# Shared decay-row buffers, 16-bit level masks and a reordered start in a DeltaNet and differential-attention block

## The chip, the cores and the metric

The kernel runs on one core of a Trainium2 chip. The metric is the device time of one execution in microseconds (us). The program is built by a scheduler: the Python code issues instructions, and the scheduler sets the order in which each engine's queue holds them, from its own estimate of when each could start. On the chip every engine takes its queue strictly in that order, so an instruction whose input is late holds up all that stands behind it on the same engine.

Engines are named as in the profile: PE (TensorE, matmuls), PEld (its weight loads), DVE (VectorE), ACT (ScalarE), POOL (GpSimd), SP (which here only issues DMAs). Names such as SPq or ACTq stand for the DMA-issuing instructions of an engine's queue.

## The reference, cut to what matters

Two layers over 256 context tokens and 256 latent tokens of width 2048. Layer 0 mixes tokens with a gated DeltaNet in both directions, layer 1 with differential attention. Each layer starts with a norm whose result is shifted and scaled by vectors that come from two large matrix products (the modulation).

```
for i in range(DEPTH):                                  # 2 layers
    mod_l = silu_c @ ada_w[i] + ada_b[i]                # shift, scale, gate: 3 x 2048
    mod_c = silu_cc @ ada_w[i] + ada_b[i]
    h_lat = rmsnorm(x, norm_w[i]) * (1.0 + sc_l) + sh_l
    h_ctx = rmsnorm(ctx, norm_w[i]) * (1.0 + sc_c) + sh_c
    ...                                                 # mixer, then x = x + gt_l * out_lat
...
lower = jnp.where(strict, jnp.einsum('nbhid,nbhjd->nbhij', kb, kc) * decay, 0.0)
tinv = lax.linalg.triangular_solve(eye + lower, ...)    # per chunk, head and direction
a_intra = jnp.einsum('nbhid,nbhjd->nbhij', qc, kc) * decay
def step(s, inp):                                       # one chunk
    v_new = u_i - w_i @ s
    o_i = q_i @ s + a_i @ v_new
    s = s * gl_i[..., None, None] + jnp.einsum('bhck,bhcv->bhkv', k_i, v_new)
```

`decay` is exp of the difference of two cumulated log gates, one per pair of tokens of a chunk. The kernel multiplies it into two kinds of matrices: k times k (to be inverted) and k times q (the attention inside a chunk).

## The kernel before, in words

**The start (lines 283 to 328).** 16 tiles of x, `xt`, 256 KB each, are loaded. ACT squares them (lines 299, 302), DVE sums them into `acc0` (line 303), `rstd_rows` (lines 203 to 214) turns the sum into a row `rrow0` by two matmuls into the psum tag `iv`, with a small power on POOL between them. The shift and scale vectors come from `ada_pair` (lines 173 to 182): 32 matmuls per pair of column blocks, over four 512 KB tiles `ar` of the modulation weight that SP loads (`ada_load`, line 169) into a ring of eight buffers; 16 pairs, 64 loads, 33.5 MB. A loop over eight steps takes two pairs, scales two tiles of x (`make_h`, lines 216 to 224: POOL, ACT, ACT, DVE), and feeds three early projections `ba`, `k0`, `q0` (lines 312 to 326). Before this stage's end SP also issues small constants and four stores that fill the DRAM scratch `tu_d` with zeros from a tile `zt` (line 466).

**The gates (`gates`, lines 361 to 457)** turn the projection `ba` into cumulated log gates, and store them as rows in DRAM, `gc_d` (line 435).

**The DeltaNet stage** works through 16 groups `g` of four states (two heads, two directions), four chunks of 128 tokens in two halves. Python generators yield in an order that a small planner (`Drive`) sets by priorities; the scheduler then orders the engines.

- `decay` (lines 682 to 695) makes a decay tile: two DMAs on SP copy rows of `gc_d` to all 128 partitions of a tile of 128 x 512 (line 686), four DVE instructions subtract and cap (line 692), one ACT instruction takes exp (line 694). It is called with the tag `grm` for the matrices to be inverted and with `gra` for the attention matrices. Each tag has one buffer, so the next load under a tag waits for line 700 of the last one.
- `scaled` (line 699: product of the matmul in psum `gq` and a mask, `gm`; line 700: times the decay tile) gives `ma` or `at`.
- `block_inv` (lines 703 to 726) inverts the diagonal 16 x 16 blocks: it stores the matrix to DRAM (`mb_d`), loads its blocks (`bk`, line 708), substitutes row by row on DVE (15 times lines 717 and 719, product `bP`, reduction into `bY`), copies the result into `TU` (tag `bT`, four copies on ACT, lines 722 and 723) and stores it with two DMAs of ACT's queue into `tu_d` (line 725).
- `stream_lev` loads `T` and `U` from `tu_d` (line 777) and doubles the blocks in three levels: a matmul into psum `iv`, a product with a level mask `lv` on DVE (`R`, line 786), two matmuls, two copies on ACT.
- `stream_b` and `steps_b` (lines 832 to 938) run the recurrence: matmuls into psum `sb` and `so` alternate with DVE and ACT instructions `y`, `yb`, `x0`, `x`, `S`, `O`.
- `filler` projects the other columns (psum `pj`) at the lowest priority, so that PE has work between the steps of the recurrence. Weights come in tiles of 256 KB on SP's queue (line 119).
- `ada_part` (lines 133 to 139) computes the other modulation columns on POOL and ACT beside all this.

**After it** come the output projection of layer 0 and layer 1. No line of the change lies there.

The tile pools: `cst` (constants, for the whole program), `gp` and `dl` (for the DeltaNet stage). Tiles with one tag share `bufs` buffers in turn: the n-th tile of a tag with three buffers is written when the readers of the tile three before it are done.

Of the kernel before, what the change touches and what calls it, by code (L numbers as in the profile page):

```python
# [10 lines left out]
F32 = mybir.dt.float32  # L11
F32R = mybir.dt.float32r
F16 = mybir.dt.float16
# [7 lines left out]
P = 128  # L21
# [40 lines left out]
def body(ctx, tc, D, d, out):  # L62
    nc = tc.nc
# [196 lines left out]
    gp_cm = pool("gp", side="right")  # L260
    gp = gp_cm.__enter__()
    gct, eg, kd, egl, lnb = (gp.tile([P, NCH, 2, HV], F32, name=n) for n in ("gct", "eg", "kd", "egl", "lnb"))
    zt = gp.tile([P, P], F16, name="zt")
    nc.vector.memset(zt, 0.0)
    t0_cm = pool("t0", reuse_waits="tile")
    t0 = t0_cm.__enter__()
    HKT = KT // 2
# [27 lines left out]
    ta = ta_cm.__enter__()  # L295
    with tc.high_priority():
        for kt in range(KT):
            nc.sync.dma_start(xt[kt], d["xT"][:, kt])
        nc.scalar.activation(acc0, xt[0], AF.Square)
        for kt in range(1, KT):  # L300
            sq = ta.tile([P, T], F32, tag="mh", name=f"sq{kt}", bufs=2)
            nc.scalar.activation(sq, xt[kt], AF.Square)
            nc.vector.tensor_tensor(acc0, acc0, sq, ALU.add)
        nc.scalar.copy(rrow0, rstd_rows(acc0, T, iv, ta.tile([P, 4, P], F32, name="rr_dg0")))
        np_ = 0
        for k0 in range(0, KT, SK):
            for kind in range(2):
                pr = kind * HKT + k0 // 2
                ada_pair(0, pr, ada_load(0, pr, ta, "ar", 8), (gq, tr)[np_ % 2](), ta)
                np_ += 1  # L310
            for kt in range(k0, k0 + 2):
                make_h((xt[kt][:, 0:256], xt[kt][:, 256:512]), kt, rrow0, 0, hhi, hl, ta, nc.gpsimd)
            for n, src, _ in EARLY:
                w = SK * P
                r = ta.tile([P, w], F32, tag="er", name=f"e{n}r{k0}", bufs=6)
                nc.sync.dma_start(r, src[:, k0 * P:k0 * P + w])
                hi = ta.tile([P, w], F32R, tag="eh", name=f"e{n}h{k0}", bufs=6)
                lo = ta.tile([P, w], F32R, tag="el", name=f"e{n}l{k0}", bufs=6)
                split(hi, lo, r)
                for k in range(SK):  # L320
                    kt, ks = k0 + k, slice(k * P, (k + 1) * P)
                    ps = early[n]
                    mm(ps, hi[:, ks], hhi[:, kt, :], kt == 0, False)
                    mm(ps, hi[:, ks], hl(kt), False, False)
                    mm(ps, lo[:, ks], hhi[:, kt, :], False, kt == KT - 1)
        ta_cm.__exit__(None, None, None)
        convw = load_small("convw", [P, 4 * KT, 5], d["convw"], gp)
        adt = load_small("adt", [P, 2, 2, HV],
                         d["adt"].to_broadcast([P, NB]).rearrange("p (k d h) -> p k d h", k=2, d=2), gp)
    t0_cm.__exit__(None, None, None)  # L330

    lv = cst.tile([P, 3, P], F32, name="lv")
    nc.sync.dma_start(lv, d["consts"][:, C_LV + 4 * P:C_LV + 7 * P].rearrange("p (l i) -> p l i", l=3))
    e16 = cst.tile([P, 16, 16], F32, name="e16")
    nc.sync.dma_start(e16, d["consts"][:, C_E16:].rearrange("p (j i) -> p j i", j=16))
    fw = load_small("fw", [P, KT], d["fw"])
# [24 lines left out]
    def gates(ps):  # L361
# [63 lines left out]
        nc.vector.tensor_tensor(g, w, wide(ea), ALU.mult)  # L425
        tri = lambda dd: cs[:, C_TRI + dd * P:C_TRI + (dd + 1) * P]
        for a in range(2):
            p3 = (gq, tr)[a]()
            for c in range(2):
                for dd in range(2):  # L430
                    q = 2 * c + dd
                    mm(p3[:HV, q * P:(q + 1) * P], g[:, 2 * a + c, dd, :], tri(dd))
            r = tl(f"r{a}", [HV, 4, P])
            nc.scalar.copy(r.rearrange("p q i -> p (q i)"), p3[:HV])
            nc.sync.dma_start(gc_d[2 * a:2 * a + 2].rearrange("c (d h) i -> h (c d) i", d=2), r)
# [23 lines left out]

    gates(early.get("ba"))  # L460

    full = lambda a: a.rearrange("u (j i) -> j u i", i=P)[:P]
    diag = lambda a: bass.AP(tensor=a[:].tensor, offset=a[:].offset, ap=[[16 * P + 16, 64], [P, 16], [1, 16]])
    for i in range(2):
# [215 lines left out]
        return t.rearrange("p (u i) -> p u i", u=4)  # L680

    def decay(g, c, s, tag):
        gr = dl.tile([P, 4, P], F32, tag=tag, name=f"{tag}{g}{c}", bufs=1)
        gsrc = gc_d[c].rearrange("(d h) i -> d h i", d=2)
        for dd in range(2):
            nc.sync.dma_start(gr[:, 2 * dd:2 * dd + 2, :],
                              gsrc[dd:dd + 1, 2 * g:2 * g + 2, :].rearrange("d h i -> d (h i)").to_broadcast([P, 2 * P])
                              .rearrange("p (h i) -> p h i", h=2))
        for u in range(4):
            dd, h = divmod(u, 2)  # L690
            j = 2 * g + h
            nc.vector.tensor_scalar(gr[:, u], gr[:, u], gct[:, c, dd, j:j + 1], lnb[:, c, dd, j:j + 1],  # L692
                                    ALU.subtract, ALU.min)
        nc.scalar.activation(gr, gr, AF.Exp)  # L694
        return gr
# [7 lines left out]
    def block_inv(g, half, m16):  # L703
# [5 lines left out]
        X = dl.tile([64, 16, 16], F32, tag="bX", name=f"bX{nm}", bufs=1)  # L709
        Y = dl.tile([64, 16, 16], F32, tag="bY", name=f"bY{nm}", bufs=1)  # L710
        pr = dl.tile([64, 16, 16], F32, tag="bP", name=f"bP{nm}", bufs=1)
        TU = dl.tile([64, 2, 16, 16], F16, tag="bT", name=f"bT{nm}", bufs=1)
        nc.vector.tensor_scalar(X[:32], bk[:32].rearrange("p j i -> p i j"), -1.0, None, ALU.mult)
        nc.vector.tensor_scalar(X[32:], bk[32:], -1.0, None, ALU.mult)
        nc.scalar.copy(Y, e16[:64])  # L715
# [585 lines left out]
```

## Time and profile before

| what | us |
| --- | --- |
| median of 3 runs (lowest, highest) | 3134.51 (3129.51, 3135.29) |
| the profiled execution, its own time | 3130.73 |
| its span, first to last instruction | 3128.9 |
| PE busy | 2817.8 |
| DVE busy | 1955.8 |
| ACT busy | 1872.4 |
| POOL busy | 2012.8 |

The table of busy times says which engine has most to do; a stage is read from the busy time inside its own window, from the list of waits there, and from the timeline of an engine around one instruction. In the profile, "idle" before an instruction is time in which its engine did nothing, and the releaser is what ended that. Window bounds are microseconds from the span's start. The start lies in 0 to 135 us, the gates up to 200 us, the DeltaNet stage up to 2050 us, the output projection and layer 1 from there on.

### The profile page before, as it was taken

How to read it: one execution, taken by the hardware profiler on the slowest of the kernel's cores; microseconds unless marked ns; L12 is line 12 of the kernel's file. 1: busy time of each engine (PE TensorE's matmuls, PEld its weight loads, DVE VectorE, ACT ScalarE, POOL GpSimd, SP SyncE). 2: the span in 40 equal slices, each digit the busy share in tenths (PEclk: the TensorE clock that was granted, in tenths of full speed). 3: DMA queues.
4: the chain of work that ended last, by engine and by line, in shares of the span. 5: the costliest groups of instructions: out<-in, count | busy, mean ns of one | idle time of the engine just before them, and what ended most of it. 6: DMA issues, size and time to landing. Idle time of an engine off the chain costs nothing. (4 is left out here: it accounts for less than half of the span.)

```text
span 3128.9 us, 52162 instructions
## 1 busy us (share of the span) xinstructions
PE 2817.8 (90%) x16178; PEld 2239.7 (72%) x16178; DVE 1955.8 (63%) x4287; ACT 1872.4 (60%) x5466; POOL 2012.8 (64%) x2370
## 2 busy tenths in 40 slices
PE   5788988988988988988898888899998999999998
PEld 2465767766766766766776666688687888888897
DVE  2178688688678677688578678632335654544454
ACT  4345766766766666766666666654556666654353
POOL 2366777777767777777777777466565666752334
PEclk8899999999999999999999999999999999999999
DMA  9646555456545545445456445667744555543345
GB/s 339 235 100 139 124 127 130 127 119 135 126 118 133 134 116 139 117 125 139 117 126 137 121 120 138 173 178 207 238 147 120 162 155 162 160 142 109 115 130 164
DMA packets 510312, 457.03 MB, mean 146 GB/s; under 512 B 241744, under 2 KB 380752, under 8 KB 510032
## 3 DMA queue, kind: packets, MB, share of 16 engines
q1 hardware_dynamic: 299456, 342.48, 37.7%
q10 hardware_dynamic: 210576, 111.22, 14.9%
q8 instruction: 127, 2.08, 0.3%
q14 instruction: 153, 1.25, 0.1%
HBM read 427.18 MB, written 26.36 MB: 145 GB/s over the span
## 5 line engine op out<-in xcount | busy, mean ns | idle before, releaser
L139 ACT ACTIVATE rp<-rp 128x256 f32<-128x256 f32 x1024 | 426.8, 417 | 298.2 <-POOL rp L138 292.6
L717 DVE TENSOR_TENSOR bP<-bX,bY 64x1 f32<-64x1 f32 (+14 forms) x480 | 225.1, 469 | 22.0 <-ACT bY L715 14.2
L139 ACT ACTIVATION_READ_ACCUMULATOR rp<-rp 128x1 f32 x1024 | 194.2, 190 | 0.0
L692 DVE TENSOR_SCALAR grm<-grm,gct,lnb 128x128 f32<-128x128 f32 x256 | 133.2, 563 | 84.8 <-DMA grm<-gc_d 84.1
L692 DVE TENSOR_SCALAR gra<-gra,gct,lnb 128x128 f32<-128x128 f32 x256 | 116.0, 493 | 85.0 <-DMA gra<-gc_d 84.7
L786 DVE TENSOR_TENSOR R<-iv,lv 128x512 f16<-128x512 f32 x192 | 127.1, 680 | 28.7 <-PE iv L83 28.5
L83 PEld LDWEIGHTS <-m 128*128 128x128 f16 x1024 | 76.2, 100 | 78.7 <-issue 71.5
L694 ACT ACTIVATE grm<-grm 128x512 f32<-128x512 f32 x64 | 40.3, 630 | 129.1 <-DVE grm L692 125.3
L719 DVE TENSOR_REDUCE bY<-bP 64x1 f32<-64x1 f32 (+14 forms) x480 | 108.6, 226 | 8.0
L750 POOL TENSOR_TENSOR ma<-ma,cs 128x512 f32<-128x512 f32 x64 | 86.5, 1352 | 32.3 <-DVE ma L700 30.0
L83 PE MATMUL iv<-T,m 128*128 128x128 f16 x768 | 74.3, 225 | 32.5 <-DMA T<-tu_d 19.1
L83 PE MATMUL iv<-U,R 128*128 128x128 f16 x768 | 76.9, 227 | 28.5 <-DVE R L786 26.4
L694 ACT ACTIVATE gra<-gra 128x512 f32<-128x512 f32 x64 | 40.4, 631 | 103.8 <-DVE gra L692 103.7
L83 PEld LDWEIGHTS <-R 128*128 128x128 f16 x768 | 48.8, 101 | 70.9 <-DVE R L786 37.9
L224 DVE TENSOR_TENSOR hlo<-mh,hhi 128x512 fp32r<-128x512 f32 x32 | 25.9, 833 | 114.9 <-ACT hhi L223 87.8
L83 PE MATMUL sb<-yb,uf 128*128 128x128 bf16 x512 | 55.5, 225 | 32.5 <-DVE yb L910 20.9
L803 ACT CAST T<-iv 128x512 f16<-128x512 f32 x128 | 74.1, 579 | 16.2 <-PE iv L83 12.5
L753 POOL TENSOR_TENSOR ml<-ma,m 128x512 bf16<-128x512 f32 x64 | 75.3, 1177 | 6.2 <-ACT m L752 5.3
L83 PEld LDWEIGHTS <-uf 128*128 128x128 f16 x512 | 36.2, 100 | 57.3 <-issue 52.1
L804 ACT CAST U<-iv 128x512 f16<-128x512 f32 x128 | 75.9, 593 | 0.0
L83 PE MATMUL so<-x,at 128*128 128x128 f32 x512 | 73.3, 280 | 0.3 <-DVE sz L966 0.3
L83 PEld LDWEIGHTS so<-x,at 128*128 128x128 f32 x512 | 67.2, 195 | 2.6 <-PE sb L83 0.4
(2767 smaller groups left out, 11393.0 us busy)
## 6 DMA issues: line engine op xcount, KB each, us to landing
aw<-in_adaw_dram ACTq DMA_DIRECT2D x512, 128.0 KB, 2.9
ar<-in_adaw_dram SPq DMA_DIRECT2D x64, 512.0 KB, 7.5
grm<-gc_d SPq DMA_DIRECT2D x128, 128.0 KB, 4.4
gra<-gc_d SPq DMA_DIRECT2D x128, 128.0 KB, 4.5
mb_d<-m ACTq DMA_DIRECT2D x32, 256.0 KB, 4.9
U<-tu_d SPq DMA_DIRECT2D x128, 64.0 KB, 2.9
T<-tu_d SPq DMA_DIRECT2D x128, 64.0 KB, 3.3
yd<-sz SPq DMA_DIRECT2D x32, 256.0 KB, 3.7
```

Of the source, the lines that this page charges most:

```text
L83: nc.tensor.matmul(o, l, r, start=start, stop=stop)
L139: nc.scalar.activation(pr, pr, AF.Copy, accum_out=acc[:, s, q:q + 1])
L224: nc.vector.tensor_tensor(hlo(kt), t, hhi[:, kt, :].bitcast(F32), ALU.subtract)
L692: nc.vector.tensor_scalar(gr[:, u], gr[:, u], gct[:, c, dd, j:j + 1], lnb[:, c, dd, j:j + 1], ALU.subtract, ALU.min)
L694: nc.scalar.activation(gr, gr, AF.Exp)
L717: nc.vector.tensor_tensor(pr[:, :i, :i], X[:, i, :i].unsqueeze(1).to_broadcast([64, i, i]), Y[:, :i, :i].rearrange("p j c -> p c j"), ALU. ...
L719: nc.vector.tensor_reduce(Y[:, i, :i], pr[:, :i, :i], AX.X, ALU.add)
L750: nc.gpsimd.tensor_tensor(ma, ma, ident.unsqueeze(1).to_broadcast([P, 4, P]), ALU.add)
L753: nc.gpsimd.tensor_tensor(ml[:, :, k], mv, m16[:, :, k], ALU.subtract)
L786: nc.vector.tensor_tensor(R, quad(pp), lvb(n), ALU.mult)
L803: nc.scalar.copy(Tm, quad(pt))
L804: nc.scalar.copy(U, quad(pu))
```

## The change

The whole diff stands below.

- The tiles of `decay` get one tag `gr` with three buffers in place of two tags with one each.
- `TU` in `block_inv` takes the tag `bP` (one buffer), which the product tile `pr` has; its own tag goes.
- The level masks `lv` become 16-bit: they are loaded as 32-bit after the gates into a tile with the tag `x`, and copied to 16 bits by ACT. The constants' load in the start goes.
- `zt` moves into the pool `dl` behind the gates, and with it the four stores that fill `tu_d` with zeros.
- The loads of x alternate between SP's and ACT's queue.
- The first two `ada_pair` calls (shift and scale of the first column blocks) stand ahead of the norm; the loop's first step leaves them out.
- In the gates the second product goes to the psum tag `iv` in place of `tr`.

```diff
--- before.py
+++ after.py
@@ -260,8 +260,6 @@
     gp_cm = pool("gp", side="right")
     gp = gp_cm.__enter__()
     gct, eg, kd, egl, lnb = (gp.tile([P, NCH, 2, HV], F32, name=n) for n in ("gct", "eg", "kd", "egl", "lnb"))
-    zt = gp.tile([P, P], F16, name="zt")
-    nc.vector.memset(zt, 0.0)
     t0_cm = pool("t0", reuse_waits="tile")
     t0 = t0_cm.__enter__()
     HKT = KT // 2
@@ -295,7 +293,9 @@
     ta = ta_cm.__enter__()
     with tc.high_priority():
         for kt in range(KT):
-            nc.sync.dma_start(xt[kt], d["xT"][:, kt])
+            (nc.sync, nc.scalar)[kt % 2].dma_start(xt[kt], d["xT"][:, kt])
+        for pr in (0, HKT):
+            ada_pair(0, pr, ada_load(0, pr, ta, "ar", 8), (gq, tr)[pr > 0](), ta)
         nc.scalar.activation(acc0, xt[0], AF.Square)
         for kt in range(1, KT):
             sq = ta.tile([P, T], F32, tag="mh", name=f"sq{kt}", bufs=2)
@@ -304,7 +304,7 @@
         nc.scalar.copy(rrow0, rstd_rows(acc0, T, iv, ta.tile([P, 4, P], F32, name="rr_dg0")))
         np_ = 0
         for k0 in range(0, KT, SK):
-            for kind in range(2):
+            for kind in range(2 if k0 else 0):
                 pr = kind * HKT + k0 // 2
                 ada_pair(0, pr, ada_load(0, pr, ta, "ar", 8), (gq, tr)[np_ % 2](), ta)
                 np_ += 1
@@ -329,8 +329,6 @@
                          d["adt"].to_broadcast([P, NB]).rearrange("p (k d h) -> p k d h", k=2, d=2), gp)
     t0_cm.__exit__(None, None, None)
 
-    lv = cst.tile([P, 3, P], F32, name="lv")
-    nc.sync.dma_start(lv, d["consts"][:, C_LV + 4 * P:C_LV + 7 * P].rearrange("p (l i) -> p l i", l=3))
     e16 = cst.tile([P, 16, 16], F32, name="e16")
     nc.sync.dma_start(e16, d["consts"][:, C_E16:].rearrange("p (j i) -> p j i", j=16))
     fw = load_small("fw", [P, KT], d["fw"])
@@ -425,7 +423,7 @@
         nc.vector.tensor_tensor(g, w, wide(ea), ALU.mult)
         tri = lambda dd: cs[:, C_TRI + dd * P:C_TRI + (dd + 1) * P]
         for a in range(2):
-            p3 = (gq, tr)[a]()
+            p3 = (gq, iv)[a]()
             for c in range(2):
                 for dd in range(2):
                     q = 2 * c + dd
@@ -459,6 +457,12 @@
 
     gates(early.get("ba"))
 
+    lv = dl.tile([P, 3, P], F16, name="lv")
+    lv32 = dl.tile([P, 3, P], F32, name="lv32", tag="x", bufs=1)
+    nc.sync.dma_start(lv32, d["consts"][:, C_LV + 4 * P:C_LV + 7 * P].rearrange("p (l i) -> p l i", l=3))
+    nc.scalar.copy(lv, lv32)
+    zt = dl.tile([P, P], F16, name="zt", tag="x0", bufs=1)
+    nc.vector.memset(zt, 0.0)
     full = lambda a: a.rearrange("u (j i) -> j u i", i=P)[:P]
     diag = lambda a: bass.AP(tensor=a[:].tensor, offset=a[:].offset, ap=[[16 * P + 16, 64], [P, 16], [1, 16]])
     for i in range(2):
@@ -680,7 +684,7 @@
         return t.rearrange("p (u i) -> p u i", u=4)
 
     def decay(g, c, s, tag):
-        gr = dl.tile([P, 4, P], F32, tag=tag, name=f"{tag}{g}{c}", bufs=1)
+        gr = dl.tile([P, 4, P], F32, tag="gr", name=f"{tag}{g}{c}", bufs=3)
         gsrc = gc_d[c].rearrange("(d h) i -> d h i", d=2)
         for dd in range(2):
             nc.sync.dma_start(gr[:, 2 * dd:2 * dd + 2, :],
@@ -709,7 +713,7 @@
         X = dl.tile([64, 16, 16], F32, tag="bX", name=f"bX{nm}", bufs=1)
         Y = dl.tile([64, 16, 16], F32, tag="bY", name=f"bY{nm}", bufs=1)
         pr = dl.tile([64, 16, 16], F32, tag="bP", name=f"bP{nm}", bufs=1)
-        TU = dl.tile([64, 2, 16, 16], F16, tag="bT", name=f"bT{nm}", bufs=1)
+        TU = dl.tile([64, 2, 16, 16], F16, tag="bP", name=f"bT{nm}", bufs=1)
         nc.vector.tensor_scalar(X[:32], bk[:32].rearrange("p j i -> p i j"), -1.0, None, ALU.mult)
         nc.vector.tensor_scalar(X[32:], bk[32:], -1.0, None, ALU.mult)
         nc.scalar.copy(Y, e16[:64])
```

The order of the engines' queues shows the moves. The first place is PE at the start of the program (`ar` with 00 to 03 and 80 to 83 are the two pairs' weight tiles, `cs,acc` is the norm's sum, `rr_dg` its row). Before:

```order
L83 MATMUL iv<-cs,acc_130 128x1 x4
L83 MATMUL gq<-ar_00_228,sc_113 32x256 x4
L83 MATMUL gq<-ar_01_234,sc_113 32x256 x4
L83 MATMUL gq<-ar_02_240,sc_113 32x256 x4
L83 MATMUL iv<-rr_dg_213,cs 128x512
L83 MATMUL gq<-ar_03_246,sc_113 32x256 x4
L83 MATMUL tr<-ar_80_259,sc_113 32x256 x4
```

After:

```order
L83 MATMUL gq<-ar_00_166,sc_111 32x256 x4
L83 MATMUL gq<-ar_01_172,sc_111 32x256 x4
L83 MATMUL iv<-cs,acc_128 128x1 x4
L83 MATMUL gq<-ar_02_178,sc_111 32x256 x4
L83 MATMUL gq<-ar_03_184,sc_111 32x256 x4
L83 MATMUL tr<-ar_80_197,sc_111 32x256 x4
L83 MATMUL iv<-rr_dg_273,cs 128x512
```

Two of the eight weight tiles now stand ahead of the norm's first matmul, and three more ahead of its second.

The second place is SP at the same time, where the zero stores stood. Before, from the last of the first eight weight tiles on:

```order
L169 DMA ar_83_277<-in_adaw_dram 128x1024
L466 DMA tu_d_88<-zt 128x8x128
L466 DMA tu_d_89<-zt 128x8x128
L466 DMA tu_d_90<-zt 128x8x128
L466 DMA tu_d_91<-zt 128x8x128
L316 DMA ebar_305<-in_wba_dram 128x256
```

After, from the last of all 64 weight tiles on:

```order
L169 DMA ar_153_1073<-in_adaw_dram 128x1024
L470 DMA tu_d_88<-zt 128x8x128
L470 DMA tu_d_89<-zt 128x8x128
L470 DMA tu_d_90<-zt 128x8x128
L470 DMA tu_d_91<-zt 128x8x128
L119 DMA g0v1r_1396<-in_win_dram 128x512
```

The four stores moved from behind eight weight tiles to behind all of them.

The third place is DVE in the middle of the DeltaNet stage, around the decay tiles of group 9 (a number behind a tile's name tells one tile from the next; `grm_14461` and `grm_14476` follow each other in one buffer). Before:

```order
L700 TENSOR_TENSOR ma_14469<-grm_14461,gm_14470 128x512
L916 TENSOR_TENSOR x_14184<-x_14077,sb 128x512
L477 SCALAR_TENSOR_TENSOR cyg9q<-pj,convw,cyg9q 128x2x255
L713 TENSOR_SCALAR bX_13957<-bk_13955 32x256
L714 TENSOR_SCALAR bX_13957<-bk_13955 32x256
L699 TENSOR_TENSOR gm_14485<-gq,cs 128x256
L692 TENSOR_SCALAR gra_14823<-gra_14823,gct,lnb 128x128 x2
L477 SCALAR_TENSOR_TENSOR cyg9q<-pj,convw,cyg9q 128x2x255
L692 TENSOR_SCALAR gra_14823<-gra_14823,gct,lnb 128x128 x2
L717 TENSOR_TENSOR bP_13959<-bX_13957,bY_13958 64x1
L692 TENSOR_SCALAR grm_14476<-grm_14476,gct,lnb 128x128 x4
```

After (`gra_15488` takes the buffer of `grm_14478`; between these two stand the tiles `gra_14825` and `gra_14837`):

```order
L696 TENSOR_SCALAR gra_14837<-gra_14837,gct,lnb 128x128 x4
L721 TENSOR_TENSOR bP_13961<-bX_13959,bY_13960 64x3x3
L704 TENSOR_TENSOR ma_14486<-grm_14478,gm_14487 128x512
L920 TENSOR_TENSOR x_14186<-x_14079,sb 128x512
L481 SCALAR_TENSOR_TENSOR cyg9q<-pj,convw,cyg9q 128x2x254
L723 TENSOR_REDUCE bY_13960<-bP_13961 64x3
L703 TENSOR_TENSOR gm_14834<-gq,cs 128x256
L481 SCALAR_TENSOR_TENSOR cyg9q<-pj,convw,cyg9q 128x2x255
L721 TENSOR_TENSOR bP_13961<-bX_13959,bY_13960 64x4x4
L696 TENSOR_SCALAR gra_15488<-gra_15488,gct,lnb 128x128 x2
```

Between the last reading of a buffer (line 700, now 704) and the first subtraction in its next content (line 692, now 696) there is still a handful of DVE's instructions: the loads moved ahead, and the subtractions moved ahead with them.

## Rows read from the trace of the kernel before

**Rows 1.** The page: busy time, share of the span and instructions of each engine.
```profile
PE 2817.8 (90%) x16178; PEld 2239.7 (72%) x16178; DVE 1955.8 (63%) x4287; ACT 1872.4 (60%) x5466; POOL 2012.8 (64%) x2370
```
**Rows 2.** Windows: busy PE, PEld, DVE, ACT, POOL (instructions), granted clock, DMA share, GB/s.
```profile
0.00:135.00 135.00, 92.06 (x672) 51.51 (x673) 21.80 (x44) 55.60 (x132) 45.25 (x64) 0.85 0.94 332
200.00:2050.00 1850.00, 1643.10 (x9596) 1273.69 (x9596) 1384.84 (x3224) 1209.63 (x3702) 1341.88 (x1662) 0.96 0.52 130
```
**Rows 3.** Windows inside the start.
```profile
15.00:20.00 5.00, 0.00 (x0) 0.00 (x0) 3.49 (x6) 3.90 (x7) 0.00 (x0) 1.00 0.66 210
35.00:40.00 5.00, 1.53 (x4) 1.17 (x4) 1.29 (x2) 4.27 (x11) 1.55 (x2) 0.67 0.85 217
50.00:100.00 50.00, 40.35 (x308) 22.50 (x312) 3.88 (x6) 20.02 (x52) 19.29 (x26) 0.80 1.00 373
```
**Rows 4.** PE's waits in 200 to 2050: us in total, times, longest.
```profile
PE iv L83 <- DVE R L786: 30.3, 26, 3.3
PE sb L83 <- DVE yb L910: 20.9, 17, 3.3
...
PE gq L83 <- DVE gm L699: 14.0, 11, 3.3
...
PE sb L83 <- DVE S L923: 9.5, 4, 3.8
...
PE sb L83 <- DVE x L916: 4.6, 8, 1.4
```
**Rows 5.** DVE's waits in 200 to 2050.
```profile
DVE gra L692 <- DMA gra<-gc_d: 84.7, 56, 4.2
DVE grm L692 <- DMA grm<-gc_d: 84.1, 50, 5.9
```
**Rows 6.** SP's timeline in the start: start, duration, line, what, count.
```profile
8.05 4.78 SPq L298 DMA_DIRECT2D xt<-in_xT_dram  x9
...
23.72 9.58 SPq L466 DMA_DIRECT2D tu_d<-zt  x4
```
**Rows 7.** DMA issues: count, KB each, median us from issue to landing.
```profile
grm<-gc_d SPq DMA_DIRECT2D x128, 128.0 KB, 4.4
...
tu_d<-bT ACTq DMA_DIRECT2D x64, 32.0 KB, 3.2
...
tu_d<-zt SPq DMA_DIRECT2D x4, 256.0 KB, 7.8
...
lv<-in_consts_dram SPq DMA_DIRECT2D x1, 192.0 KB, 5.6
```
**Rows 8.** DVE by line and shape, 200 to 2050: count, busy, mean ns, idle before.
```profile
L786 DVE TENSOR_TENSOR R<-iv,lv 128x512 f16<-128x512 f32 x192 | 127.1, 680 | 28.7 <-PE iv L83 28.5
...
L916 DVE TENSOR_TENSOR x<-x,sb 128x512 f32<-128x512 bf16 x62 | 42.0, 677 | 33.3 <-PE sb L83 31.6 <-ACT g2qhi L185 1.6
```
**Rows 9.** DVE's timeline at the first decay tiles.
```profile
207.19 1.45 DVE L692 TENSOR_SCALAR grm<-grm,gct,lnb 128x128 f32<-128x128 f32 x2 [3.93 <-DMA grm<-gc_d]
209.38 0.60 DVE L692 TENSOR_SCALAR grm<-grm,gct,lnb 128x128 f32<-128x128 f32 x2 [0.75 <-DMA grm<-gc_d]
```
**Rows 10.** Windows: the first 100 us of the DeltaNet stage.
```profile
200.00:300.00 100.00, 79.91 (x372) 57.87 (x372) 80.56 (x178) 53.11 (x152) 73.74 (x85) 0.93 0.58 130
```
**Rows 11.** ACT's and DVE's timeline at the end of block inversions, first pair and last.
```profile
241.88 0.38 DVE L719 TENSOR_REDUCE bY<-bP 64x15 f32<-64x225 f32 x1
...
245.66 0.15 DVE L717 TENSOR_TENSOR bP<-bX,bY 64x1 f32<-64x1 f32 x1
...
244.43 0.62 ACTq L725 DMA_DIRECT2D tu_d<-bT  x1
...
1936.78 0.38 DVE L719 TENSOR_REDUCE bY<-bP 64x15 f32<-64x225 f32 x1
1940.82 0.15 DVE L717 TENSOR_TENSOR bP<-bX,bY 64x1 f32<-64x1 f32 x1 [1.75 <-ACT bY L715]
...
1939.60 0.72 ACTq L725 DMA_DIRECT2D tu_d<-bT  x1
```

## The prediction

> **What bounds the kernel now.** Read first the busy times [rows 1]: PE is busy 90% of the span, and no other engine over 64%. The change leaves PE's matmuls as they are, so only PE's idle time, 3128.9 - 2817.8 = 311 us, can go or grow. Read next where it lies [rows 2]: 135 - 92 = 43 us in the start, and 1850 - 1643 = 207 us in the DeltaNet stage, the two places that the change touches.
>
> In the start PE is not the limit. The DMA engines are busy 0.94 of it and 1.00 between 50 and 100 us, at 373 GB/s [rows 2, 3]. Two stretches fall short: 15 to 20 us with 210 GB/s, and 35 to 40 us with 217 GB/s. So this stage is paid in bytes and in holes between transfers.
>
> In the DeltaNet stage the list of PE's waits [rows 4] shows many short waits at places where PE's queue reached a matmul before DVE had made its input: five groups, 30.3 + 20.9 + 14.0 + 9.5 + 4.6 = 79 us. DVE itself is idle 1850 - 1385 = 465 us of this stage, and 84.7 + 84.1 = 169 us of that is waiting for decay rows from DRAM [rows 5]. Both queues are in order, so a DVE that waits for a row also delays the `R`, `yb` and `S` that stand behind it. I put the exchange at 79/465 = 0.17 us of PE per us of DVE's idle time; its ends are 0 (the fillers cover it) and 1.
>
> **The start: fewer bytes, fewer holes.** The four zero stores (4 x 256 KB) and the masks' load (192 KB, [rows 7]) leave the stage: 1.24 MB, at 373 GB/s 3.3 us. They go to the time of the gates, in which DMA has room. SP spent 9.58 us at the zero stores [rows 6], with the early projections' loads and the ninth weight tile behind them; that, and PE at the norm, made the hole at 35 to 40 us. The holes are worth 5 x (373 - 210)/373 = 2.2 and 5 x (373 - 217)/373 = 2.1 us. In PE's new order two weight tiles are consumed ahead of the norm, so ring buffers come free earlier, but the small constants that made the first hole are still issued between weight tiles. I take 3.3 plus half of the holes: **5 us** won; the ends are 0 (PE's and POOL's steps set the pace after all) and 8. Of the two pairs that move, all eight loads, 32 matmuls each, copies and fills move along; PE was waiting for the norm then, so they cost nothing new. If the norm came later by some us, PE's 20% of idle time between 50 and 100 us [rows 3] would take it up.
>
> The second queue for x: nine issues took SP 4.78 us [rows 6], about half a us each, while the memory was already saturated. It frees some 4 us of SP's time, no bandwidth, and this is in the term above. The Trainium skill speaks against this part (DMA: Bandwidth & Descriptors, "Issuing engines are not separate DMA queues"): DMAs run on the same 16 engines whatever engine issues them, so a second issuer saves issue time only. The saturated stretch agrees; no row here has both queues loading at once. If only this counted, the start would be as long as before, which is a rival below.
>
> **Three shared decay buffers.** One would expect the 169 us to go: a load may now run ahead by three tiles. The order of DVE's queue says otherwise. I added up, with mean durations of the trace, DVE's work between the last reading of a buffer (line 700) and the first subtraction in its next content (line 692). Before, the median over 126 such places is 3.3 us, and a load takes 4.4 us to land [rows 7]; summing 4.4 less the work, where positive, gives 165 us, close to the 169 us that DVE did wait [rows 5]. So this sum can be trusted. In the changed order, with the buffer counted three tiles back, the median is 3.5 us and the same sum is 146 us. The scheduler used the buffers to make decay tiles earlier (from first subtraction to last reading there lie now 30 us of DVE's work, before 10), but still places each subtraction just behind its load. DVE's waits shrink by 165 - 146 = 19 us, not by 169; at 0.17 that is **3 us** for PE. Ends: 0, and 169 x 0.17 = 29 if all went.
>
> At the stage's beginning it counts directly. DVE stood 3.93 + 0.75 us for the second decay tile of group 0 [rows 9], with nothing else in flight, on the way to the first inversion. Now three tiles are loaded at once. PE was idle 20 us in these 100 us [rows 10], where the stage's mean is 11. I take **3 us** won, between 0 and 4.7.
>
> **TU in the buffer of the product.** This adds a wait. The next inversion's first product (line 717) must wait until the stores of `TU` have landed; before, it needed only the copies. In 17 places the two halves' inversions follow each other closely; the first and last are [rows 11]. First: last reduction ends at 242.26, second store issues at 244.43, plus 3.2 to land [rows 7] is 247.63; the next product started at 245.66, so it would be 1.97 us later. Last: 1936.78 + 0.38, then 1939.60 + 3.2 = 1942.80 against 1940.82, 1.98 us. Over all 17 these shortfalls sum to 23 us (two are zero). On DVE's queue `R`, `y`, `S` and the convolutions stand behind that product, and PE waits for these [rows 4]. At 0.17 this costs **4 us**; ends 0 and 23, if each us reaches PE.
>
> **Edits at nothing.** 16-bit masks: `R` takes 680 ns with 32-bit masks [rows 8], and `x`, which reads psum and a 16-bit tile already, takes 677 ns, so 16 bits beside psum save nothing. The masks' load and copy happen once, between the gates and the first `R`; about 6 us uncovered [rows 7, 8], but the first inversion lies in front of that. `iv` for `tr` in the gates: PE's list of waits names no wait for that buffer; 0, and a few us either way if the order of the gates' copies changes. The rest of the program has the same instructions in nearly the same order: 0.
>
> **Sum.** -5 - 3 - 3 + 4 = -7 us. The profiled execution took 3130.7 us, which makes 3123.7, say **3124 us**. That execution was 3.8 us below the median of the runs, 3134.5; against the median 3124 is 0.34% less. The ends add to -8 - 4.7 - 29 = -42 (3089) and +23 (3154).
>
> **Rivals.**
>
> *The waits for decay rows go after all* (chance 0.18). The tiles are ready 30 us before they are read, so the scheduler had room, and on the chip a load that is issued early may be early. Then -29 in place of -3: 3124 - 26 = 3098 us. Against it: the sum above, which met the old waits within 3%, finds 88 places instead of 95 with less than 4.4 us of work.
>
> *The inversion becomes the bound* (0.20). The new wait stands once per group between the halves, and the second half's inversion gates the levels, then the recurrence. If PE has nothing to put in there, the 23 us arrive whole, and nothing but the start is won: 3130.7 - 5 + 23 = 3149 us, slower. It decides if the next product's wait for the store is over 1.5 us in most groups and PE's waits for `R` and `T` rise with it. Against it: fillers keep PE at 89% in this stage [rows 2].
>
> *The start stays* (0.20). By the rule named above two queues bring nothing; and if the ring of weight tiles was paced by PE (busy 40 of 50 us between 50 and 100 us at a granted clock of 0.80 [rows 3]), fewer bytes bring nothing either. Then 3124 + 5 = 3129 us: no change that can be told.
>
> **How the numbers follow.** The forecast itself has 0.42, with a range of its own of 3114 to 3134: a new order of all queues shifts some waits by chance. A measurement of this kernel can tell 0.2%, 6.3 us: faster is below 3128, slower above 3141. Faster: 0.29 of the forecast, 0.18, and 0.03 of the third rival, 0.50. The same: 0.12 of the forecast and 0.15 of the third rival, 0.27. Slower: 0.01, 0.20 and 0.02, 0.23. The range: 3094 leaves out some of the first rival, 3146 half of the second, together 2 in 10.
>
> **What would show it.** In the changed profile: the last weight tile's transfer ends near 126 us instead of 131; no zero store before 130 us; DVE's waits for decay rows sum to some 150 us; a new group, the product `bP` waiting for the DMA that stores `TU`, of 15 to 30 us; `R` at 680 ns; PE idle in the DeltaNet stage 200 to 210 us. Wrong if the waits for rows fall under 80 us, if the product's wait exceeds 40 us, or if PE's idle time in that stage moves by more than 15 us.

## The result and the profile after

The changed kernel takes 3156.01 us (median of 4 runs, 3148.23 to 3160.83) against 3134.53: ratio 1.0070, 95% interval 1.0044 to 1.0095. It is slower by 22 us, where 3124 was forecast with 3146 as the upper end. The profiled execution took 3159.29 us, its span is 3157.5.

In the start the holes closed, as forecast. The page's busy times and the windows of the changed kernel, to be held against [rows 1 to 3]:

```profile
PE 2818.9 (89%) x16178; PEld 2241.9 (71%) x16178; DVE 1946.8 (62%) x4287; ACT 1870.8 (59%) x5467; POOL 2014.6 (64%) x2370
```
```profile
15.00:20.00 5.00, 0.19 (x4) 0.22 (x8) 4.38 (x7) 3.83 (x7) 0.00 (x0) 1.00 1.01 353
35.00:40.00 5.00, 3.19 (x20) 1.65 (x13) 1.29 (x2) 4.65 (x12) 3.80 (x6) 0.55 1.06 371
200.00:2050.00 1850.00, 1617.26 (x9438) 1248.35 (x9437) 1363.98 (x3186) 1192.54 (x3647) 1322.39 (x1642) 0.96 0.52 127
```

The two holes are filled, 353 and 371 GB/s where 210 and 217 stood. PE's busy time is as before; its idle time went from 311 to 338.6 us (span less busy time). The whole loss lies in the DeltaNet stage: in 200 to 2050 PE is idle 233 us instead of 207. The inversion's first product starts at 214.3 instead of 223.1 us and its last at 1998.5 instead of 1965.1, as its row in the view by tile shows (duration min/median/max in ns, first and last start in us):

```profile
L717 DVE TENSOR_TENSOR bP<-bX,bY x480: 140/474/1337, 223.1 to 1965.1; 64x1 f32<-64x1 f32 x32, 64x16 f32<-64x16 f32 x32, 64x49 f32<-64x49 f32 x32, 64x100 f32<-64x100 f32 x32
```
```profile
L721 DVE TENSOR_TENSOR bP<-bX,bY x480: 139/459/1458, 214.3 to 1998.5; 64x1 f32<-64x1 f32 x32, 64x16 f32<-64x16 f32 x32, 64x49 f32<-64x49 f32 x32, 64x100 f32<-64x100 f32 x32
```

So 8.8 us were won up to there, and 42.2 lost between the two (1742.0 to 1784.2 us). Below, "PE's waits in the stage" are the sum of PE's list of waits between these two starts: 189.5 before, 221.1 after. The waits of the changed kernel in 200 to 2050, PE's and DVE's, against [rows 4, 5] (lines have moved by 4):

```profile
PE sb L83 <- DVE yb L914: 33.6, 17, 4.1
PE iv L83 <- DVE R L790: 30.7, 27, 4.8
PE iv L83 <- DMA T<-tu_d: 22.9, 17, 3.8
PE sb L83 <- ACT yb L888: 18.7, 10, 3.5
PE gq L83 <- DVE gm L703: 17.1, 12, 4.2
```
```profile
DVE grm L696 <- DMA grm<-gc_d: 92.8, 66, 4.1
DVE gra L696 <- DMA gra<-gc_d: 74.7, 53, 4.8
...
DVE bP L721 <- DMA tu_d<-bT: 26.6, 10, 4.7
```

DVE's waits for decay rows did not fall at all: 94.1 + 74.7 = 168.8 us over the span, where 84.7 + 84.1 = 168.8 stood; that the tenths agree is chance. The loads themselves took longer to land, 4.9 us for `grm` where 4.4 stood [rows 7] (count, KB each, median us from issue to landing):

```profile
grm<-gc_d SPq DMA_DIRECT2D x128, 128.0 KB, 4.9
gra<-gc_d SPq DMA_DIRECT2D x128, 128.0 KB, 4.4
```

The new wait of the product for `TU`'s store is there, 26.6 us. And the `yb` of the recurrence reaches PE later: 33.6 us where 20.9 stood. One such place, first on PE, then on DVE (start, duration, what; in brackets the idle time before it and its releaser):

```profile
896.22 0.22 PE L83 MATMUL sb<-x,ml 128*128 128x128 bf16 x1
...
900.14 0.39 PE L83 MATMUL pj<-hlo,g7khi 128*128 128x512 f32 x1
904.68 0.58 PE L83 MATMUL sb<-yb,uf 128*128 128x128 bf16 x4 [4.14 <-DVE yb L914]
```
```profile
898.16 0.17 DVE L723 TENSOR_REDUCE bY<-bP 64x6 f32<-64x36 f32 x1
899.09 1.64 DVE L696 TENSOR_SCALAR grm<-grm,gct,lnb 128x128 f32<-128x128 f32 x2 [0.75 <-DMA grm<-gc_d]
900.65 0.41 DVE L703 TENSOR_TENSOR gm<-gq,cs 128x256 f32<-128x256 f32 x1
900.98 0.44 DVE L721 TENSOR_TENSOR bP<-bX,bY 64x49 f32<-64x49 f32 x1
901.35 0.59 DVE L696 TENSOR_SCALAR grm<-grm,gct,lnb 128x128 f32<-128x128 f32 x2
901.86 0.19 DVE L723 TENSOR_REDUCE bY<-bP 64x7 f32<-64x49 f32 x1
902.90 1.13 DVE L696 TENSOR_SCALAR grm<-grm,gct,lnb 128x128 f32<-128x128 f32 x2 [0.85 <-DMA grm<-gc_d]
903.95 0.67 DVE L914 TENSOR_TENSOR yb<-y,sb 128x512 bf16<-128x512 f32 x1
```

`yb`'s input left PE at 896.44, yet DVE reaches it at 903.95: ahead of it stand, beside shorter work, two waits for decay rows and six subtractions of tiles that are needed much later (the first is read at 957.0). PE's filler runs out after 900.14, and PE stands 4.14 us.

### The profile page after: what moved, and what is told of

Same layout as the page of the kernel before. It is cut to its first block, busy times and chain, and to the rows that moved or that the text cites. A ratio compares the mean times of both kernels' runs of the same rounds, so it can differ in the third digit from the quotient of the medians.

```text
span 3157.5 us, 52146 instructions
## 1 busy us (share of the span) xinstructions
PE 2818.9 (89%) x16178; PEld 2241.9 (71%) x16178; DVE 1946.8 (62%) x4287; ACT 1870.8 (59%) x5467; POOL 2014.6 (64%) x2370
## 5 line engine op out<-in xcount | busy, mean ns | idle before, releaser
L721 DVE TENSOR_TENSOR bP<-bX,bY 64x1 f32<-64x1 f32 (+14 forms) x480 | 221.0, 460 | 56.5 <-DMA tu_d<-bT 26.6
L696 DVE TENSOR_SCALAR grm<-grm,gct,lnb 128x128 f32<-128x128 f32 x256 | 123.3, 522 | 94.8 <-DMA grm<-gc_d 94.1
L696 DVE TENSOR_SCALAR gra<-gra,gct,lnb 128x128 f32<-128x128 f32 x256 | 125.4, 532 | 75.2 <-DMA gra<-gc_d 74.7
L83 PE MATMUL sb<-yb,uf 128*128 128x128 bf16 x512 | 54.1, 223 | 52.5 <-DVE yb L914 33.6
L83 PE MATMUL iv<-T,m 128*128 128x128 f16 x768 | 74.0, 225 | 30.1 <-DMA T<-tu_d 22.9
```

Source lines behind the costliest of these rows:

```text
L83: nc.tensor.matmul(o, l, r, start=start, stop=stop)
L721: nc.vector.tensor_tensor(pr[:, :i, :i], X[:, i, :i].unsqueeze(1).to_broadcast([64, i, i]), Y[:, :i, :i].rearrange("p j c -> p c j"), ALU. ...
```

## The experiments

Each ratio is against the kernel before on the same chip. "Rows" is DVE's whole wait for decay rows, "TU" the product's wait for the store.

| run | decay buffers | TU's buffer | ratio [95%] | rows, us | TU, us |
| --- | --- | --- | --- | --- | --- |
| before | 2 tags x 1 | own | 1 | 168.8 | |
| after | 3 shared | product's | 1.0070 [1.0044, 1.0095] | 168.8 | 26.6 |
| e1 | 2 x 1 | product's | 1.0044 [1.0024, 1.0063] | 136.4 | 38.7 |
| e2 | 2 x 1 | product's | 1.0007 [0.9991, 1.0022] | 157.1 | 11.3 |
| e3 | 2 x 1 | own | 0.9993 [0.9980, 1.0006] | 141.1 | |
| e4 | 3 shared | own | 1.0033 [1.0012, 1.0053] | 149.0 | |
| e5 | 2 x 1 | own | 1.0003 [0.9986, 1.0020] | 128.1 | |
| e6 | 2 shared | own | 0.9973 [0.9956, 0.9990] | 133.3 | |
| e7 | 3 shared | product's | 1.0098 [1.0078, 1.0119] | 162.2 | 30.7 |
| e8 | 2 x 1 | own | 0.9986 [0.9974, 0.9998] | 155.4 | |
| e9 | 2 shared | own | 0.9980 [0.9965, 0.9996] | 142.8 | |
| e10 | 2 shared | own | 0.9948 [0.9931, 0.9965] | 150.5 | |
| e11 | 3 shared, queued 2 back | own | 0.9778 [0.9755, 0.9801] | 8.1 | |
| e12 | 2 shared, queued 1 back | own | 0.9814 [0.9796, 0.9831] | 9.1 | |
| e13 | 3 shared, queued 2 back | product's | 0.9888 [0.9869, 0.9908] | 10.7 | 17.8 |
| e14 | 3 shared, queued 1 back | own | 0.9796 [0.9774, 0.9819] | 0 | |

**e1: the kernel before with `TU` in the product's buffer.**

```
-        TU = dl.tile([64, 2, 16, 16], F16, tag="bT", name=f"bT{nm}", bufs=1)
+        TU = dl.tile([64, 2, 16, 16], F16, tag="bP", name=f"bT{nm}", bufs=1)
```

> The kernel before with one edit: TU takes the product's buffer (tag bP). Theory A (the wait of the next inversion's product for the stores of TU made the change slow): DVE waits 20 to 30 us for these stores, the time rises by 15 to 30 us over the kernel before, to 3150 to 3165 us. Theory B (the decay tiles that share three buffers did it): the same wait of 20 to 30 us on DVE, but the time stays within 8 us of 3134 us. Theory C (any edit that makes the scheduler order the queues anew moves the time by some tens of us, whatever its content): anything from 3115 to 3160 us, without a relation to DVE's waits.

1.0044: slower. TU's place alone costs some 14 us here, beside a wait of 38.7 us; that is just under theory A's 15 to 30 us and above theory B's 8.

**e2, e3: the changed kernel with the decay tags of before; e3 also with `TU` in its own buffer.**

```
-        gr = dl.tile([P, 4, P], F32, tag="gr", name=f"{tag}{g}{c}", bufs=3)
+        gr = dl.tile([P, 4, P], F32, tag=tag, name=f"{tag}{g}{c}", bufs=1)
```

> The changed kernel, decay tiles with two tags of one buffer each as before; TU still in the product's buffer. Theory A: still slow, 3145 to 3160 us, with the wait for TU's stores at 20 to 30 us. Theory B: the loss goes, 3120 to 3132 us. Theory C: anything from 3110 to 3160 us.

> The changed kernel without its two edits in the buffers of the DeltaNet stage: decay tiles with two tags, TU in its own buffer. What is left is the start, the 16-bit masks, the later zero stores and the psum tag in the gates. Theories A and B: the start's 5 us are won, 3120 to 3132 us. Theory C: anything from 3110 to 3160 us.

1.0007 and 0.9993. Without the three shared buffers nearly the whole loss is gone, as theory B has it: e2 differs from the changed kernel in these buffers alone, and they cost 0.63%, 20 us. TU's place costs 0.14% here, beside a wait of 11.3 us, but the intervals of e2 and e3 overlap, so this is not clear of noise.

**e4: the changed kernel with `TU` in its own buffer.** To make room, the unit matrix `e16` is 16-bit, the square's scrap `jk` bf16, and the decay table `adt` shares the buffer of `bX`; the loads of `e16` and `adt` move behind the start with that ("space savings").

```
-        TU = dl.tile([64, 2, 16, 16], F16, tag="bP", name=f"bT{nm}", bufs=1)
+        TU = dl.tile([64, 2, 16, 16], F16, tag="bT", name=f"bT{nm}", bufs=1)
```

> The changed kernel with TU in its own buffer; three shared decay buffers stay. To find the space, the 16 x 16 identity is kept in 16 bits, a scratch tile of squares in 16 bits, and the gates' constants in a tile that the inversion uses later. Theory A: no wait for TU's stores, the loss goes, 3120 to 3132 us. Theory B: still slow, 3145 to 3160 us. Theory C: anything from 3110 to 3160 us.

1.0033: three shared buffers lose without TU's wait too, by as much as the lower end of theory B's range (3145 us is 1.0033 of 3134.5).

**e5: the kernel before with another psum tag in the gates,** which moves DVE's instructions at some hundreds of places and changes nothing else.

```
-            p3 = (gq, tr)[a]()
+            p3 = (gq, iv)[a]()
```

> The kernel before with one edit: the gates' second product goes to the psum tag iv in place of tr. It touches no resource of the DeltaNet stage after its first microseconds, but the scheduler orders DVE's queue anew at some 350 places. Theory B2 (three shared decay buffers cost 10 to 20 us by their own working): within 6 us of the kernel before. Theory C (a new order alone moves the time by 10 us and more): over 8 us away from the kernel before, in either direction.

1.0003: this new order by itself did not move the time, though its rows' wait is 41 us shorter. It is one order of many.

**e6: the kernel before with both kinds of decay rows in two shared buffers.**

```
-        gr = dl.tile([P, 4, P], F32, tag=tag, name=f"{tag}{g}{c}", bufs=1)
+        gr = dl.tile([P, 4, P], F32, tag="gr", name=f"{tag}{g}{c}", bufs=2)
```

> The kernel before with decay tiles of both kinds in two shared buffers, the same space as before. Theory B1 (sharing is what costs: a load for one kind waits until a tile of the other kind is used up): slower, by 10 us or more, since with two shared buffers this coupling is stronger than with three; DVE's waits for decay rows over 200 us. Theory B2' (running ahead is what costs: subtractions made early stand in front of the recurrence on DVE): within 6 us of the kernel before, as two buffers give no more tiles than before. Theory C: anywhere within 15 us.

0.9973: faster, by 8 us, a little more than theory B2' allowed. Sharing is not what costs.

**e7: the changed kernel with e4's space savings, `TU` in the product's buffer.**

> The changed kernel with the space-saving edits of the earlier run (16-bit identity, 16-bit scratch, the gates' constants in another tile), TU still in the product's buffer, three shared decay buffers. It differs from that run in TU's buffer alone. If TU's buffer costs 4 to 14 us beside the shared decay buffers: 0.15 to 0.45% above the ratio of that run (1.003), 1.005 to 1.008. If only the order decides: anything between 0.998 and 1.010.

1.0098; against e4, TU's place costs 0.65% beside three shared buffers, more than the 0.15 to 0.45% expected.

**e8: the kernel before with the changed start (x on two queues, first pairs ahead of the norm).**

```
-            nc.sync.dma_start(xt[kt], d["xT"][:, kt])
+            (nc.sync, nc.scalar)[kt % 2].dma_start(xt[kt], d["xT"][:, kt])
+        for pr in (0, HKT):
+            ada_pair(0, pr, ada_load(0, pr, ta, "ar", 8), (gq, tr)[pr > 0](), ta)
...
-            for kind in range(2):
+            for kind in range(2 if k0 else 0):
```

> The kernel before with the start's two moves alone: x on two queues, the first two modulation pairs ahead of the norm. The zero stores and the masks' load stay where they were. If the start is paced by transfers: the last weight tile lands 2 to 4 us earlier, the time falls by as much, 0.999. If the zero stores were the main part of the start's gain: no change, 1.000. Theory C: anything between 0.996 and 1.005.

0.9986: these two moves win 4.4 us, between 0.6 and 8. The zero stores and the masks' load are still in the start here. Of the two holes the first is filled and the second hardly, which goes with the zero stores that the forecast named for it:

```profile
15.00:20.00 5.00, 0.20 (x4) 0.23 (x8) 4.38 (x7) 3.46 (x7) 0.00 (x0) 1.00 1.04 363
35.00:40.00 5.00, 2.29 (x5) 1.64 (x6) 1.29 (x2) 4.08 (x10) 2.30 (x3) 0.69 0.89 241
```

**e9, e10: two shared buffers in the changed kernel, `TU` in its own; e10 with e4's space savings, so that it differs from e4 in this number alone.**

```
-        gr = dl.tile([P, 4, P], F32, tag="gr", name=f"{tag}{g}{c}", bufs=3)
+        gr = dl.tile([P, 4, P], F32, tag="gr", name=f"{tag}{g}{c}", bufs=2)
```

> The changed kernel with two shared decay buffers in place of three, and TU in a buffer of its own; the start, the masks and the gates as changed. Theory (the third buffer and TU's place are the two costs, sharing and the start are gains): the gains of two shared buffers (0.9973) and of the start (0.9986) add up, 0.994 to 0.997 of the kernel before; DVE's waits for decay rows 120 to 150 us, PE's waits in the DeltaNet stage at or under 185. Rival (sharing wins only by the order it happened to give): as with two separate buffers, 0.998 to 1.001.

> The changed kernel with TU in its own buffer and the space savings, exactly as in the run with three shared buffers (1.0033), but with two shared buffers: one number differs. Theory (it is the third buffer that costs): 0.995 to 0.999, so 0.4 to 0.8% under the run with three. Rival (the space savings, that is the 16-bit unit matrix, the bf16 square rows and the decay table in a shared buffer, made that run slow): 1.002 to 1.004 again.

e10: 0.9948, 0.85% below e4, with the same wait for rows (150.5 and 149.0 us). So the third buffer costs without making DVE wait longer, as far as one profile of each kernel tells (e4's profiled execution took 3126.8 us, its median is 3137.9). e9: 0.9980, less than the two gains together and within its rival's range: against e3, which differs in these buffers alone, two shared buffers win 0.13%, and the intervals overlap. So whether sharing wins by more than its order is open. The space savings, which should be neutral, won 0.3% here and lost 0.3% from after to e7. Single steps add up no better than that, and the third buffer's price carries the same uncertainty.

**e11: e4 with the subtractions held back.** They are queued on DVE behind the product that reads the tile two earlier; loads still run three ahead.

```
         for u in range(4):
...
+            with tc.issue_after(used[-2]) if len(used) > 1 else nullcontext():
                 nc.vector.tensor_scalar(gr[:, u], ...)
...
-        nc.vector.tensor_tensor(o.rearrange(...), gr.rearrange(...), ...)
+        i = nc.vector.tensor_tensor(o.rearrange(...), gr.rearrange(...), ...)
+        used.append(getattr(i, "ins", i))
```

> Three shared buffers, TU in its own buffer, space savings as before; but the four subtractions of a decay tile are queued on DVE behind the product that reads the tile two earlier, so the loads run three tiles ahead while the subtractions run two ahead. By the sum of this document DVE's waits for decay rows fall from 142 to under 40 us, and DVE's work between subtraction and product from 29 to some 19 us (median). Theory (subtractions that run ahead stand in front of the recurrence): the third buffer's 0.4% go, 0.999 or less; if each us of DVE's wait gives PE 0.17 us back, another 0.5%, 0.992 to 0.996. Rival 1 (DVE's waits for rows are cover that costs nothing): rows' waits fall, but other waits take their place and the time stays 0.998 to 1.004. Rival 2 (the third buffer's loads or space cost, wherever the subtractions stand): 1.003 or more.

0.9778, far under every kernel so far, and 2.5% under e4, from which it differs in the queueing alone. The expectation had 0.992 to 0.996: right in direction, too small by far. DVE's costliest groups, e10's and then e11's (busy us, mean ns, idle before, releaser):

```profile
L698 DVE TENSOR_SCALAR grm<-grm,gct,lnb 128x128 f32<-128x128 f32 x256 | 117.2, 500 | 87.7 <-DMA grm<-gc_d 87.5
L698 DVE TENSOR_SCALAR gra<-gra,gct,lnb 128x128 f32<-128x128 f32 x256 | 127.4, 539 | 63.3 <-DMA gra<-gc_d 63.0
```
```profile
L702 DVE TENSOR_SCALAR gra<-gra,gct,lnb 128x128 f32<-128x128 f32 x256 | 176.2, 737 | 0.2 <-DMA gra<-gc_d 0.2
L702 DVE TENSOR_SCALAR grm<-grm,gct,lnb 128x128 f32<-128x128 f32 x256 | 150.5, 640 | 8.0 <-DMA grm<-gc_d 7.9
```

PE's waits for `yb`, `R`, `T` and `gm`, e10's and then e11's, over the span:

```profile
PE sb L83 <- DVE yb L916: 28.3, 20, 3.9
...
PE iv L83 <- DVE R L792: 18.0, 19, 2.8
...
PE iv L83 <- DMA T<-tu_d: 11.7, 16, 2.8
...
PE gq L83 <- DVE gm L705: 7.6, 7, 2.2
```
```profile
PE gq L84 <- DVE gm L709: 32.7, 25, 4.2
...
PE sb L84 <- DVE yb L921: 16.7, 10, 4.1
PE iv L84 <- DVE R L797: 12.5, 16, 2.7
PE iv L84 <- DMA T<-tu_d: 8.7, 11, 1.9
```

The waits for rows are gone, PE's waits in the stage fall from 179.4 to 146.8 us (e4: 194.1), and of these four only that for `gm`, which stands beside the held-back work, has grown. Rivals 1 and 2 of the expectation are out.

**e12, e13, e14: the same queueing elsewhere.** e12 is e9 with the subtractions behind the product one tile back (`used[-1]`), e14 is e4 with that, e13 is the changed kernel with e11's edit alone.

> The changed kernel with two shared decay buffers, TU in its own buffer, no space savings, and the subtractions of a decay tile queued behind the product before it (one tile back). By the order DVE's waits for rows sum to 4 us, and the work between subtraction and product has a median of 7 us. Theory W (the waits for rows are what costs): as the run with three buffers and the same queueing two back, 0.975 to 0.981. Theory L (the lead of the subtractions costs as well): faster still, 0.966 to 0.974. Rival (too late: exponential and product now stand right behind the subtractions, and DVE waits for ACT): 0.982 or more, with new waits of the products for ACT's exponential over 40 us.

> The changed kernel as it is, TU in the product's buffer and all, with one edit: the subtractions of a decay tile are queued behind the product that reads the tile two earlier. DVE's waits for rows fall from 169 us to under 30. If TU's place costs what it did (0.65% beside three buffers): 0.978 plus 0.0065, 0.982 to 0.987. Rival (TU's place cost only because DVE was short of slack through the waits for rows): 0.976 to 0.981.

> Three shared buffers, TU in its own buffer, space savings, subtractions queued behind the product one back: loads three ahead, subtractions one ahead (median 8 us of DVE's work before their product). If only waits and lead count, the third buffer brings nothing here: within 0.3% of the run with two buffers and the same queueing. If loads that run further ahead still help or hurt, it differs by more.

e12 and e14 agree within their intervals (0.9814, 0.9796): with the waits gone the third buffer brings nothing that can be told. e12 lies between theory W and the rival by its time, but its waits for ACT's exponential are 6.5 us and not over 40. Nor does it pay to make the tiles later: between a subtraction and its product lie 19 us of DVE's work (median) in e11, 8 in e14 and in e12, and e11 is not slower than the others, so theory L is out for leads of that size; the changed kernel's lead of 29 us was not run without the waits. In e13 the changed kernel turns from 1.0070 to 0.9888 by the queueing alone, but stays 1.1% behind e11 and misses the 0.982 to 0.987 expected: TU's place still costs, and more than expected, though e13's waits for rows are short too:

```profile
DVE bP L726 <- DMA tu_d<-bT: 17.8, 7, 4.2
DVE grm L700 <- DMA grm<-gc_d: 8.0, 9, 2.3
DVE gra L700 <- DMA gra<-gc_d: 2.7, 4, 1.2
```

(e13 lacks e11's space savings, so some 0.3% of this may be theirs.)

## Why the prediction was wrong, point by point

**The start, 5 us won: right in the trace, its size in time open.** SP issues the last modulation weight tile at 118.7 instead of 126.4 us, and it lands at 126.6 instead of 133.2; the zero stores go out from 140.5 us on, after this stage. In time, e3 has the whole changed start without the two edits of buffers and wins 2 us, between a loss of 2 and a gain of 6. e8's 4.4 us are those of the two moves alone, for which the forecast had counted half of the holes, 2 us; the 3.3 us for the bytes that leave are measured by no run. By the Trainium skill's rule (DMA: Bandwidth & Descriptors, "Issuing engines are not separate DMA queues") a second issuer saves issue time only; e8 agrees in so far as it filled a hole between transfers, but no run tells the second queue from the moved pairs. The rival that the start stays is out in the trace; in time e8's interval shuts it out by little, and e3's does not.

**The 16-bit masks, nothing: right.** `R` takes 679 ns, 680 before [rows 8].

**Three shared buffers, 3 us won by shorter waits: wrong in size and sign.** The step that failed is "DVE's waits shrink by 165 - 146 = 19 us ... at 0.17". They stayed at 168.8. With 3 us here and 3 at the stage's beginning the three buffers were to win 6 us; they cost 0.63% (20 us) where they were the only difference (e2 to after). At the stage's beginning, up to 225 us, DVE's waits for rows of `grm` fell from 7.1 to 4.5 us, yet in 200 to 300 PE is idle 22 us, 20 before [rows 10]. The order was read rightly: the same sum over the changed kernel's own trace, with 4.4 us for a landing, gives 144 us where the text has 146. But the loads took longer to land, 4.9 us on the mean over both kinds where 4.6 stood, and each subtraction still stands just behind its load. The third buffer alone cost 0.85% (26 us; e10 to e4), beside equal waits, so the sum of the waits does not tell the price. The text had seen that tiles would be made 30 us ahead instead of 10; it counted how long DVE waits and not in front of whom. That the subtractions' place in DVE's queue decides is shown by e13, where moving them alone turns the loss into a gain. How much comes from PE standing behind these waits is not shown: PE's idle times that ended with DVE and in which a wait for rows fell sum to 15.3 us before, 34.6 in the changed kernel, 23.2 in e10, 31.4 in e4 and none in e11, but also to 26.4 in e3, which is no slower than the kernel before. The rest of the third buffer's price is not taken apart by any run.

**The exchange, 0.17 us of PE's idle time per us of DVE's wait: of the right size for idle time, too low for the time.** The pairs that differ in the queueing alone are after to e13, e9 to e12, e4 to e11 and e4 to e14; the waits that went are 158, 134, 141 and 149 us. Per us of them PE's idle time in the profiles fell by 0.29, 0.10, 0.33 and 0.30 us, and the time (ratios times some 3123 us) by 0.36, 0.39, 0.57 and 0.50. What lies between is PE's busy time, of which the last section tells. Nor is this the price of any wait for rows: in e5 another order took 41 us of them away, and the time stayed. 0.17 came from dividing five of PE's waits by all of DVE's idle time, of which some 159 us in this stage are DVE waiting for PE.

**The waits for rows go after all (0.18, 3098 us): not here.** But its price of 26 us was also too low: e11 and e14 stand 69 and 64 us under the kernel before, PE's shorter busy time included. The waits could have gone, only not by a buffer: the scheduler spent it on an earlier subtraction.

**`TU` in the product's buffer, 4 us lost: wait right, price too low.** Forecast 23 us of wait, found 26.6. The price was 0.14% (e2 to e3, not clear of noise), 0.44% (e1), 0.65% (e4 to e7) and 1.1% (e11 to e13, some 0.3% of it perhaps the space savings'), 4 to 34 us: at the bottom the forecast, at the top its upper end of 23 and more. The rival that the inversion becomes the bound (0.20, 3149 us) was nearest to the result by its number, and that is luck: with `TU` in the product's buffer and the decay tags of before (e2) the time is that of the kernel before. Its sign of PE's waits for `T` rising showed (19.1 to 22.9 us between the two starts), that for `R` did not (30.3 to 30.7).

**The sum.** Start -0.14% (e8), sharing -0.27% (e6), third buffer +0.85%, TU +0.65%: +1.1% against +0.70% measured. The last two steps were taken with the space savings and end at e7, which stands at +0.98%, so most of the difference from the changed kernel is the 0.3% that separates the two. The bound named for PE's idle time in the stage, 15 us, was passed, with 26.

## What to carry to other kernels

Count a wait by what stands behind it in its queue, and not by its length: here a us of DVE waiting for a row gave back 0.36 to 0.57 us where the queueing took it away, and nothing where another order did (e5). A further buffer didn't cure the wait, since the scheduler moved the consumer forward with the load; holding the consumer back behind a later instruction, so that the load has time to land, won 1.7 to 2.5%, where the buffers, a merged tile and a new start had lost 0.7%. A tile whose store must land, put into the buffer of the next round's first write, cost up to 0.65% where nothing else differed.

## What was not expected of the hardware

The subtractions of a decay tile got slower when the waits ahead of them went: 500 and 539 ns on the mean in e10, 640 and 737 in e11, and DVE's busy time rose from 1954.9 to 2038.8 us. Laid over POOL's timeline, those of which over half lies beside POOL's work take 0.71 us on the mean in e10 and 0.77 in e11, the others 0.34 and 0.33; 254 of 512 lie so in e10, 419 of 512 in e11. The Trainium skill has a rule that would fit (SBUF — State Buffer, "Who interferes with whom": VectorE's two-port modes and GpSimd lock each other out of a shared pair of ports for a whole instruction); the trace agrees in that one beside POOL's work takes twice as long, but no run here shows the mode or kept POOL away. So part of what the shorter waits give is taken back.

PE's busy time fell too. The page's busy times of e4, of e11 and of e14:

```profile
PE 2815.5 (90%) x16178; PEld 2245.5 (72%) x16178; DVE 1967.2 (63%) x4287; ACT 1870.7 (60%) x5468; POOL 2009.7 (64%) x2370
```
```profile
PE 2787.6 (91%) x16178; PEld 2227.1 (73%) x16178; DVE 2038.8 (67%) x4287; ACT 1867.6 (61%) x5468; POOL 2022.2 (66%) x2370
```
```profile
PE 2804.0 (91%) x16178; PEld 2238.5 (73%) x16178; DVE 2044.3 (67%) x4287; ACT 1866.6 (61%) x5468; POOL 2018.6 (66%) x2370
```

With the same matmuls PE is busy 28 us less in e11 than in e4, at a mean granted clock of 0.972 instead of 0.961: of the 74 us between these two spans, 28 are shorter matmuls and 46 less idle time. The prediction's "only PE's idle time can go or grow" missed that. It does not follow from less idle time alone: in e14's profile PE is idle as little as in e11's (265 and 263 us), but the clock is 0.964 and PE is busy 16 us longer; in e3's it is idle 313 us, as before, at a clock of 0.971, and busy 2798.6 us. The clock also differs between executions of one kernel: 0.959 to 0.968 in the 28 of the kernel before that go with e1 to e4, 0.964 to 0.973 in e14's five. On the mean it was 0.970 to 0.973 in the four kernels with the queueing and 0.962 in the kernel before; why is open.
